# A two-layer decoder trunk on one core: the rests of the summed activations made by GpSimd instead of VectorE

## The chip, the cores and the metric

The kernel runs on one core of one Trainium2 chip. The metric is the device time of one execution in microseconds (us); a time is the median of several runs. Engine names are those of the profile: PE is TensorE, DVE is VectorE, ACT is ScalarE, POOL is GpSimd, SP is SyncE (it only issues DMAs here).

## The reference, cut to what matters

```python
D_MODEL, SEQ, DEPTH, D_FF = 1024, 512, 2, 2816

def short_conv_mixer(h, w_in, conv_w, w_out):
    b_gate, c_gate, u = jnp.split(h @ w_in, 3, axis=-1)
    y = b_gate * causal_depthwise_conv3(c_gate * u, conv_w)
    return y @ w_out

def swiglu(h, w_gate_up, w_down):
    g, u = jnp.split(h @ w_gate_up, 2, axis=-1)
    return (jax.nn.silu(g) * u) @ w_down

def reference(x, ...):
    for l in range(DEPTH):
        if l == 0:   # short convolution layer
            mix = short_conv_mixer(rmsnorm(h, a_pre_norm[l]), a_w_in[l], a_conv_w[l], a_w_out[l])
            h = h + rmsnorm(mix, a_post_norm[l])
        else:        # sliding-window attention over a shared K/V, then
            h = h + rmsnorm(attn, b_post_norm[j])
        ff = swiglu(rmsnorm(h, ffn_pre_norm[l]), ffn_w_gate_up[l], ffn_w_down[l])
        h = h + rmsnorm(ff, ffn_post_norm[l])
    return h
```

Everything is float32. 512 tokens pass through a gated convolution, a SwiGLU, an attention and a second SwiGLU.

## The kernel before, in words

**Products in three parts.** A float32 operand is written as a leading part (`hi`, in TensorE's reduced float format) and a rest (`lo` = value minus `hi`). A product is the sum of three matmuls: `hi*lo`, `hi*hi`, `lo*hi` (`mm3`, L193 to L195). So every weight tile is read from memory as `raw` (128x1024), copied by ACT to `whi` (L478) and subtracted by DVE to `wlo` (L479). Activations are split in the same way.

**Stages.** The convolution layer (to about 175 us of the trace), the first SwiGLU (about 175 to 510), the attention (to about 675), the second SwiGLU (to the end). In a SwiGLU the gate and up matrices are worked through two feature tiles at a time, a *gate pair*: a first pair in plain form and then ten in each layer, here called q0 to q9, with four down projections among them: d0 behind q2, d1 behind q4, d2 behind q6, d3 behind q9.

**A gate pair** is a fast 2x2 block product with seven products instead of eight, in the order 1, 2, 6, 5, 7, 3, 4, each a *job* with a 128x1024 weight tile. Products 1, 6, 7 and 4 accumulate in the same two banks of PSUM (`gx`, L1076 and L1079), 5 in `gz`, 3 in `gv`, 2 in `gy`. After each of them `take` (L1034) adds the bank into the running sums `st`; the next product of the `gx` chain may not start before the adds on the banks have read them. For some weights the summed blocks are made by POOL's DMAs in device memory (`hsum`, L547); in pairs q1 to q5 and q7 DVE makes two of them itself (`raw`, L466).

**The activations of a pair.** The finished pair `gr` (silu times up) goes through `pair_sums`: DVE makes the four sums of blocks `s` (L593, L594), and `split` writes each of two `s` tiles and one half of `gr` as `ahi` and `alo` (128x512 each), the stationary operands of the later down projection. The same function serves the first four column groups of the convolution's output (there the source is `yy`). In each SwiGLU the plain pair and q0 to q7 go this way (q8 and q9 go another), each during the pair that follows it; with two calls in the convolution that makes 20 calls of `pair_sums` and 60 of `split`.

**The order on each engine** is the order in which the code is written (`manual_schedule` over PE, DVE, ACT and POOL): engines take their instructions strictly in that order and wait for each other by semaphores. `in_line` runs a job's products, prepares the weights three jobs ahead (`LINE_LEAD`), and then lets one *late* step go, such as one `split` of the pair before. `issue` puts POOL's DMAs between, each held back until a named ACT copy is done ("pace").

Of the kernel before, what the change touches and what calls it, by code (L numbers as in the profile page):

```python
# [10 lines left out]
F32 = mybir.dt.float32  # L11
F32R = mybir.dt.float32r
AF = mybir.ActivationFunctionType
ALU = mybir.AluOpType
# [60 lines left out]
def yoco_kernel(  # L75
# [22 lines left out]
    nc = tc.nc  # L98
# [19 lines left out]
    def slot(s, dt=F32, w=S):  # L118
        return big.tile([P, w], dt, tag="slot", name=name(s), padded_shape=[P, S])
# [457 lines left out]
    def pair_sums(gr, to):  # L577
        v = gr.rearrange("p (k r i c) -> p k r i c", k=2, r=2, i=2)
        a11, a21, a12, a22 = v[:, 0, :, 0], v[:, 0, :, 1], v[:, 1, :, 0], v[:, 1, :, 1]
        sums = [slot("s") for _ in range(2)]  # L580
        s1, s2, s3, s4 = (p[:, c : c + 256].rearrange("p (r c) -> p r c", r=2)
                          for p in sums for c in (0, 256))
        e = slot("a11", F32R)
        h, lo = (e[:, c : c + 256].rearrange("p (r c) -> p r c", r=2) for c in (0, 256))
        t = [(e[:, :256], e[:, 256:])]
        to.append(t)

        def first():
            nc.scalar.activation(h, a11, AF.Copy)
            nc.vector.tensor_tensor(out=lo, in0=a11, in1=h.bitcast(F32), op=ALU.subtract)  # L590

        def add(p, q, u, v, w):
            nc.vector.tensor_tensor(out=p, in0=u, in1=v, op=ALU.subtract)  # L593
            nc.vector.scalar_tensor_tensor(out=q, in0=p if w is a11 else s2, scalar=-1.0,  # L594
                                           in1=w, op0=ALU.mult, op1=ALU.subtract)

        def split(src):
            hi, lo = slot("ahi", F32R), slot("alo", F32R)
            nc.scalar.activation(hi, src, AF.Copy)
            nc.vector.tensor_tensor(out=lo, in0=src, in1=hi.bitcast(F32), op=ALU.subtract)  # L600
            t.append((hi, lo))

        parts = [first, lambda: add(s1, s2, a22, a21, a11), lambda: add(s3, s4, a11, a21, a12)]
        return parts + [lambda src=src: split(src) for src in (*sums, gr[:, S:])]
# [855 lines left out]
    with tc.manual_schedule(engines=ALL):  # L1460
# [67 lines left out]
        src = [p.rearrange("p (h d) -> p h d", d=HD) for p in pv]  # L1528
        for j in range(NB):
            nc.scalar.activation(dst[j][0], src[j], AF.Copy)  # L1530
        for j in range(NB):
            if j == 2:
                qs[0].split(nc.vector)
            nc.vector.tensor_tensor(out=dst[j][1], in0=src[j], in1=dst[j][0].bitcast(F32),
                                    op=ALU.subtract)

    with tc.manual_schedule(engines=ALL):
        sum_on("a0")
        for i in range(KT + 2):
# [9 lines left out]
            for c in order.split():  # L1549
# [9 lines left out]
                op, n = c[0], [int(d) for d in c[1:].rstrip("-")]  # L1559
# [130 lines left out]
```

## Time and profile before

| | |
|---|---|
| median of three runs | 1019.07 us (1019.07 to 1019.42) |
| the profiled execution | 1018.79 us, of which 1017.0 us lie between its first and last instruction |
| granted TensorE clock | 0.999 |
| busy: PE, DVE, ACT, POOL | 1006.7, 893.3, 582.8, 195.2 us |
| idle time of PE that ends with a wait for DVE | 2.2 us on `gx`, in six places |

The table's busy times are unions over each engine's instructions. A matmul's end is modelled, so a PE that waits for a fraction of a microsecond can still read as busy; the distance between the starts of equal products shows such a wait better. Times in the trace count from the first instruction.

### The profile page before, as it was taken

To read this page: it belongs to the slowest core of one execution; us is meant where nothing else is said; L and a number is where in the kernel's file an instruction comes from. 1 tells how busy PE (TensorE), PEld (TensorE's weight loads), DVE (VectorE), ACT (ScalarE), POOL (GpSimd) and SP (SyncE) were. 2 spreads that over 40 slices of the span, in tenths; PEclk is the share of its full clock that TensorE was granted. 3 is DMA by queue.
4 is the path that set the end of the run, shared out by engine and by line. 5 is a ranking of instruction groups with operands and counts; after the bars stand their busy time and mean duration, and the time that the engine had idled before them with its cause. 6 is when DMAs were issued, how large, how long until landed. Compare 5 with 4: busy or idle time off the path is not lost.

```text
span 1017.0 us, 16055 instructions
## 1 busy us (share of the span) xinstructions
PE 1006.7 (99%) x5848; PEld 884.2 (87%) x5848; DVE 893.3 (88%) x1540; ACT 582.8 (57%) x1055; POOL 195.2 (19%) x259
## 2 busy tenths in 40 slices
PE   9999999999999999999999999999999999999997
PEld 7888888998889898898898888889988888989986
DVE  5766767899889999999888998778997999999996
ACT  7322444875656465566485786677656564655641
POOL 0443033112101011000032754131111010110001
PEclk9999999999999999999999999999999999999999
DMA  9897689549979789769504889976889677979742
GB/s 359 292 263 226 183 248 343 163 166 273 337 233 287 246 287 313 244 212 339 199 1 143 210 252 262 290 238 150 279 281 313 181 238 224 301 274 269 249 166 83
DMA packets 66575, 244.50 MB, mean 240 GB/s; under 512 B 7872, under 2 KB 8384, under 8 KB 54720
## 3 DMA queue, kind: packets, MB, share of 16 engines
q1 hardware_dynamic: 51328, 145.98, 38.7%
q0 software_dynamic: 14592, 96.48, 37.4%
q10 hardware_dynamic: 576, 1.02, 0.3%
q8 instruction: 46, 0.75, 0.3%
q14 instruction: 33, 0.27, 0.1%
HBM read 237.15 MB, written 102.76 MB: 334 GB/s over the span
## 4 chain that ended last, share of the span: by engine, by line
PE 89%; DVE 8%; issue 2%; DMA 0%; DVEq 0%; SPq 0%; ACT 0%; ACTq 0%
PE gx L1076 12%; PE gx L1079 6%; PE pcub L194 4%; PE pcub L195 4%; PE pcub L193 4%; PE px L194 4%; PE px L193 4%; PE px L195 4%; PE gz L1076 3%; PE pmix L194 3%; PE pmix L193 3%; PE pmix L195 3%; DVE wlo L479 2%; PE pz L195 2%; PE pz L194 2%
## 5 line engine op out<-in xcount | busy, mean ns | idle before, releaser
L479 DVE TENSOR_TENSOR wlo<-raw,whi 128x1024 fp32r<-128x1024 f32 x225 | 274.6, 1225 | 28.8 <-ACT whi L478 28.7
L478 ACT ACTIVATE whi<-raw 128x1024 fp32r<-128x1024 f32 x225 | 233.5, 1051 | 98.2 <-DVE raw L466 29.0
L1076 PE MATMUL gx<-xt,whi 128*128 128x512 f32 x480 | 121.6, 395 | 2.2 <-DVE st L1034 2.2
L1076 PEld LDWEIGHTS gx<-xt,whi 128*128 128x128 f32 x480 | 86.1, 189 | 19.7 <-DVE st L1034 1.7
L547 POOL DMA_DIRECT2D hsum<-in_w_gb_dram x96 | 62.9, 736 | 151.0 <-ACT whi L478 101.8
L547 POOL DMA_DIRECT2D hsum<-hsum x32 | 25.4, 793 | 296.0 <-ACT whi L478 246.4
L1034 DVE TENSOR_TENSOR st<-gx,st 128x256 f32<-128x256 f32 x200 | 77.5, 419 | 2.2 <-ACT st L1054 0.4
L1054 ACT ACTIVATE st<-gx 128x256 f32<-128x256 f32 x120 | 43.1, 380 | 60.8 <-PE gx L1079 57.6
L1079 PEld LDWEIGHTS gx<-xt,wlo 128*128 128x128 f32 x480 | 65.4, 190 | 4.8
L1079 PE MATMUL gx<-xt,wlo 128*128 128x256 f32 x480 | 66.9, 282 | 0.0
L1090 ACT ACTIVATE gr<-gr 128x1024 f32<-128x1024 f32 x20 | 21.2, 1062 | 63.6 <-DVE gr L1034 63.6
L193 PE MATMUL px<-wlo,ahi 128*128 128x512 f32 x120 | 46.7, 389 | 0.0
L194 PE MATMUL px<-whi,ahi 128*128 128x512 f32 x120 | 46.7, 389 | 0.0
L195 PE MATMUL px<-whi,alo 128*128 128x512 f32 x120 | 46.7, 389 | 0.0
L195 PE MATMUL gv<-xhi,wlo 128*128 128x256 f32 x160 | 45.3, 283 | 0.0
L193 PE MATMUL gy<-xlo,whi 128*128 128x256 f32 x160 | 45.3, 283 | 0.0
L194 PE MATMUL gy<-xhi,whi 128*128 128x256 f32 x160 | 45.3, 283 | 0.0
L193 PE MATMUL gv<-xlo,whi 128*128 128x256 f32 x160 | 45.3, 283 | 0.0
L195 PE MATMUL gy<-xhi,wlo 128*128 128x256 f32 x160 | 45.3, 283 | 0.0
L194 PE MATMUL gv<-xhi,whi 128*128 128x256 f32 x160 | 45.2, 283 | 0.0
L547 POOL DMA_DIRECT2D hsum<-in_w_dn_dram x48 | 31.7, 754 | 46.5 <-ACT whi L478 31.3
L1076 PE MATMUL gz<-xt,whi 128*128 128x512 f32 x160 | 40.1, 392 | 0.0
(298 smaller groups left out, 2923.5 us busy)
## 6 DMA issues: line engine op xcount, KB each, us to landing
hsum<-in_w_gb_dram POOLq DMA_DIRECT2D x96, 512.0 KB, 7.8
raw<-hsum SPq DMA_DIRECT2D x88, 512.0 KB, 8.1
raw<-in_w_gb_dram SPq DMA_DIRECT2D x60, 512.0 KB, 7.2
hsum<-in_w_dn_dram POOLq DMA_DIRECT2D x36, 512.0 KB, 8.2
raw<-in_w_dn_dram SPq DMA_DIRECT2D x32, 512.0 KB, 6.2
hsum<-hsum POOLq DMA_DIRECT2D x28, 512.0 KB, 5.7
raw<-in_w_in_dram SPq DMA_DIRECT2D x21, 512.0 KB, 7.9
hsum<-in_w_dn_dram POOLq DMA_DIRECT2D x12, 768.0 KB, 11.8
```

The costliest lines, as they stand in the source:

```text
L193: nc.tensor.matmul(out, whi, xlo, start=start, stop=False, **kw)
L194: nc.tensor.matmul(out, whi, xhi, start=False, stop=False, **kw)
L195: nc.tensor.matmul(out, wlo, xhi, start=False, stop=stop, **kw)
L478: self.begun = nc.scalar.activation(hi[:, :n], raw, AF.Copy)
L479: nc.vector.tensor_tensor(out=lo[:, :n], in0=raw, in1=hi[:, :n].bitcast(F32), op=ALU.subtract)
L547: nc.gpsimd.dma_start(dst, src, max_dma_last_dim=4 * 4 * S, **kw))
L1034: nc.vector.tensor_tensor(out=out, in0=a, in1=b, op=ALU.add)
L1054: nc.scalar.activation(ste, a, AF.Copy)
L1076: nc.tensor.matmul(banks[c][e], whi[:, kk], factors[p][k][2], start=opened and k == 0, stop=False, **kw)
L1079: nc.tensor.matmul(banks[c][e][:, :256], wlo[:, kk], factors[p][k][0], start=False, stop=k == 3 and p in (4, 5), **kw)
L1090: nc.scalar.activation(kept[2], kept[2], AF.Silu)
```

## The change

One instruction of `split` in `pair_sums` moves from DVE's queue to POOL's:

```diff
         def split(src):
             hi, lo = slot("ahi", F32R), slot("alo", F32R)
             nc.scalar.activation(hi, src, AF.Copy)
-            nc.vector.tensor_tensor(out=lo, in0=src, in1=hi.bitcast(F32), op=ALU.subtract)
+            nc.gpsimd.tensor_tensor(out=lo, in0=src, in1=hi.bitcast(F32), op=ALU.subtract)
             t.append((hi, lo))
```

The rows of PE, ACT and SP stay as they were. DVE has 60 rows less, POOL 60 more.

DVE while pair q1 of the first SwiGLU is worked on (`gx`, `gv`, `gz` are its banks in PSUM; the `alo` are the rests of the pair finished before it, q0; `wlo` and `raw` belong to jobs still to come), with the removed rows marked:

```order
 L1034 TENSOR_TENSOR st_451_2236<-st_452_2237,st_451_2236 128x512
 L479 TENSOR_TENSOR wlo_470_2362<-raw_426_2076,whi_469_2361 128x1024
-L600 TENSOR_TENSOR alo_473_2369<-s_448_2233,ahi_472_2368 128x512
 L1034 TENSOR_TENSOR st_452_2237<-gx_454_2239,st_452_2237 128x256 x2
 L1034 TENSOR_TENSOR st_452_2237<-gx_455_2240,st_452_2237 128x256 x2
 L479 TENSOR_TENSOR wlo_475_2393<-raw_429_2105,whi_474_2392 128x1024
-L600 TENSOR_TENSOR alo_477_2398<-s_449_2234,ahi_476_2397 128x512
 L1034 TENSOR_TENSOR gr_453_2238<-gv_478_2401,st_451_2236 128x2x256
 L479 TENSOR_TENSOR wlo_480_2428<-raw_434_2137,whi_479_2427 128x1024
 L466 TENSOR_TENSOR raw_429_2105<-raw_429_2105,raw_463_2327 128x1024
-L600 TENSOR_TENSOR alo_482_2434<-gr_417_2014,ahi_481_2433 128x512
```

The four adds on `gx` now follow the `wlo` directly, and the other steps close up in the same way.

POOL at the same place (`hsum` are the sums of weight blocks in device memory):

```order
 L547 DMA hsum_25_146<-in_w_gb_dram 64x2048
 L547 DMA hsum_26_147<-in_w_gb_dram 64x2048
+L600 TENSOR_TENSOR alo_473_2369<-s_448_2233,ahi_472_2368 128x512
 L547 DMA hsum_27_148<-in_w_gb_dram 64x2048
+L600 TENSOR_TENSOR alo_477_2398<-s_449_2234,ahi_476_2397 128x512
 L547 DMA hsum_28_149<-in_w_gb_dram 64x2048
+L600 TENSOR_TENSOR alo_482_2434<-gr_417_2014,ahi_481_2433 128x512
 L547 DMA hsum_25_146<-in_w_gb_dram 64x2048
```

POOL's queue held only paced DMAs here; the three subtractions now stand between them, and two DMAs stand behind a subtraction that they did not have to pass.

POOL in the convolution (`yy` is the gated output of two column groups, `cut` the product that the taps are taken from):

```order
 L772 TENSOR_TENSOR yy_172_534<-cut_170_532,bry_171_533 128x512
 L772 TENSOR_TENSOR yy_172_534<-cut_174_543,bry_175_544 128x512
+L600 TENSOR_TENSOR alo_188_607<-s_176_552,ahi_187_606 128x512
+L600 TENSOR_TENSOR alo_194_643<-s_177_553,ahi_193_642 128x512
+L600 TENSOR_TENSOR alo_196_647<-yy_172_534,ahi_195_646 128x512
 L759 TENSOR_TENSOR cut_180_556<-cru_179_555 128x512
```

The next column group's `cut` now has three subtractions ahead of it in POOL's queue.

## Prediction

> **What bounds the kernel now.** I read the page first (busy time, the chain that ended last), then busy time by stage, then the starts of equal products on PE, then DVE's rows in the one place where PE's starts slip.
>
> ```profile
> PE 1006.7 (99%) x5848; PEld 884.2 (87%) x5848; DVE 893.3 (88%) x1540; ACT 582.8 (57%) x1055; POOL 195.2 (19%) x259
> PE 89%; DVE 8%; issue 2%; DMA 0%; DVEq 0%; SPq 0%; ACT 0%; ACTq 0%
> 60.00:100.00 40.00, 40.00 (x179) 33.11 (x177) 26.40 (x32) 9.82 (x12) 12.41 (x15) 1.00 0.85 241
> 229.00:250.40 21.40, 20.54 (x131) 18.24 (x129) 21.23 (x36) 12.34 (x20) 4.65 (x8) 1.00 0.94 295
> 353.00:391.50 38.50, 38.50 (x253) 35.29 (x252) 37.15 (x62) 23.67 (x38) 5.21 (x8) 1.00 0.84 263
> ```
>
> The last three rows are stretches: length, then busy PE, PEld, DVE, ACT, POOL with counts, the granted clock, DMA share, GB/s. PE sets the time almost everywhere. In the convolution (60 to 100) DVE is busy for two thirds. In q5 and q6 (353 to 391.5) PE is full and DVE keeps 38.50 - 37.15 = 1.35 us free in two pairs. Only in q1 (229 to 250.4) is it the other way round: DVE 21.23 of 21.40, PE with gaps. How much PE loses there shows in the start of product 4:
>
> ```profile
> 220.56 0.40 PE L1076 MATMUL gx<-xt,whi 128*128 128x512 f32 x1
> 241.00 2.09 PE L1076 MATMUL gx<-xt,whi 128*128 128x512 f32 x8 [0.20 <-DVE st L1034]
> 262.31 2.09 PE L1076 MATMUL gx<-xt,whi 128*128 128x512 f32 x8 [0.20 <-DVE st L1034]
> 369.18 0.40 PE L1076 MATMUL gx<-xt,whi 128*128 128x512 f32 x1
> 388.90 0.40 PE L1076 MATMUL gx<-xt,whi 128*128 128x512 f32 x1
> 740.04 0.47 PE L1076 MATMUL gx<-xt,whi 128*128 128x512 f32 x1 [0.20 <-DVE st L1034]
> 761.35 0.47 PE L1076 MATMUL gx<-xt,whi 128*128 128x512 f32 x1 [0.21 <-DVE st L1034]
> ```
>
> From q5 to q6 it is 388.90 - 369.18 = 19.72 us, PE's own pace. From q0 to q1 it is 20.44, from q1 to q2 21.31: PE loses 0.72 + 1.59 = 2.31 us to DVE. The second layer repeats it (761.35 - 740.04 = 21.31). So 4.6 us in all can be won by a lighter DVE, and no more; elsewhere a lighter DVE buys nothing.
>
> **The change, part by part.** What goes from DVE and what comes to POOL (columns: count, shortest/median/longest in ns; and count, busy us, mean ns):
>
> ```profile
> L600 DVE TENSOR_TENSOR alo<-s,ahi x40: 683/685/693, 49.0 to 947.2; 128x512 fp32r<-128x512 f32 x40
> L1285 POOL TENSOR_TENSOR rhl<-ra,rhl 128x512 fp32r<-128x512 f32 x7 | 9.5, 1364 | 9.4 <-ACT rhl L1284 9.3
> ```
>
> The same subtraction of the same shape exists on POOL, in the attention: 1.36 us for 0.685. Sixty of them are 60 x 1.36 = 82 us on an engine that is busy for 195 of 1017, and 60 x 0.685 = 41 us less on DVE. The direct cost on POOL is nothing as long as nobody waits for its queue, which I come to below. The indirect one is larger: the two engines hinder each other.
>
> ```profile
> 66.61 2.33 DVE L479 TENSOR_TENSOR wlo<-raw,whi 128x1024 fp32r<-128x1024 f32 x1 [0.17 <-ACT whi L478]
> 66.58 1.29 POOL L759 TENSOR_TENSOR cut<-cru 128x512 f32<-128x512 f32 x1 [5.84 <-DVE cru L758]
> 53.10 1.22 DVE L479 TENSOR_TENSOR wlo<-raw,whi 128x1024 fp32r<-128x1024 f32 x1
> 53.32 2.16 POOL L759 TENSOR_TENSOR cut<-cru 128x512 f32<-128x512 f32 x1 [6.15 <-issue]
> 115.31 1.28 DVE L648 TENSOR_TENSOR mix<-mix,pz 128x512 f32<-128x512 f32 x2
> 116.50 1.42 DVE L479 TENSOR_TENSOR wlo<-raw,whi 128x1024 fp32r<-128x1024 f32 x1
> 115.54 1.30 POOL L772 TENSOR_TENSOR bry<-cut,bry 128x512 f32<-128x512 f32 x1 [13.40 <-DVE bry L771]
> ```
>
> A `wlo` that begins 0.03 us behind a POOL product takes 2.33 us instead of 1.22: it stands still for 1.11 us, until 1.14 us after POOL's start. A POOL product that begins 0.22 us behind a `wlo` takes 2.16 instead of 1.29: it stands still for 0.87, until 0.13 us before the `wlo` ends. Two adds with one operand in PSUM (`mix`, `pz`) run beside POOL at 0.68 each, unhindered; the `wlo` behind them waits 0.20. So whoever is first holds the other off, if DVE reads both operands from SBUF (`wlo`, `raw`, `s`, `st<-st`), and not if it reads one from PSUM (the adds on `gx`, `gz`, `gv`). The Trainium skill ("SBUF — State Buffer", section "SBUF: two separate sides") states just this as an exclusive lock on a shared port pair, held for the whole instruction; the trace agrees, with 1.11 and 0.87 us. By that rule alone, every moved subtraction shuts DVE out for longer than the 0.685 us that it took there, and the sum would turn against the change; that is the first rival below. What the rows add is that much of DVE's work has an operand in PSUM, beside which POOL costs nothing.
>
> So I walk one pair, q1, where it counts.
>
> ```profile
> 236.19 0.62 ACT L599 ACTIVATE ahi<-s 128x512 fp32r<-128x512 f32 x1
> 236.59 0.52 POOL L547 DMA_DIRECT2D hsum<-in_w_gb_dram  x1 [1.01 <-ACT whi L478]
> 236.85 0.75 DVE L1034 TENSOR_TENSOR st<-gz,st 128x256 f32<-128x256 f32 x2
> 237.63 0.69 DVE L1034 TENSOR_TENSOR st<-st,st 128x512 f32<-128x512 f32 x1
> 237.66 0.62 ACT L599 ACTIVATE ahi<-s 128x512 fp32r<-128x512 f32 x1
> 238.05 0.50 POOL L547 DMA_DIRECT2D hsum<-in_w_gb_dram  x1 [0.93 <-ACT whi L478]
> 238.24 1.22 DVE L479 TENSOR_TENSOR wlo<-raw,whi 128x1024 fp32r<-128x1024 f32 x1
> 239.13 0.62 ACT L599 ACTIVATE ahi<-gr 128x512 fp32r<-128x512 f32 x1
> 239.37 0.68 DVE L600 TENSOR_TENSOR alo<-s,ahi 128x512 fp32r<-128x512 f32 x1
> 239.98 1.67 DVE L1034 TENSOR_TENSOR st<-gx,st 128x256 f32<-128x256 f32 x4
> 241.56 1.22 DVE L479 TENSOR_TENSOR wlo<-raw,whi 128x1024 fp32r<-128x1024 f32 x1
> 242.69 0.69 DVE L600 TENSOR_TENSOR alo<-s,ahi 128x512 fp32r<-128x512 f32 x1
> 243.29 0.68 DVE L1034 TENSOR_TENSOR gr<-gv,st 128x512 f32<-128x512 f32 x1
> 243.89 1.22 DVE L479 TENSOR_TENSOR wlo<-raw,whi 128x1024 fp32r<-128x1024 f32 x1
> ```
>
> Removed from DVE's row of work: 239.98 - 239.37 = 0.61 us each, three times, 1.82 us a pair. Added, with 1.14 us of hold each:
> - The first subtraction may begin when `ahi` is done (236.81) and the DMA ahead of it issued (237.11). It falls into the adds on `gz`, holds the port until some 238.3, and `st<-st`, due at 237.63, waits 0.7 us. If DVE is earlier by then, the subtraction waits for `st<-st` and the `wlo` behind it pays 1.1.
> - The second finds the `wlo` running, waits for it, and then lies beside the four adds on `gx` (1.58 us): no wait. The 0.50 us DMA ahead of it keeps it off the port until that `wlo` is under way.
> - The third finds the next `wlo` running and then lies beside `gr<-gv` (0.60 us): the `wlo` behind that waits about 0.4.
>
> That is 1.1 to 1.5 us of waits for 1.82 saved: DVE gains 0.7 to 0.3 us in a pair. Ahead of the last slip of a layer (product 4 of q2) lie the three rests made in q0, the three in q1 and the first in q2. I take 0.7 for q0 (nothing has shifted yet), 0.3 for q1 (DVE is 0.7 earlier, the dearer case), and for the first in q2 0.61 less a wait between 0 and 0.8, so 0.2 as the middle: 1.2 us a layer, of 2.31 that can be won, 2.4 in both. The ends: waits of nothing give 4.6; waits of 1.11 for each give 7 x (1.11 - 0.61) = 3.5 us a layer of loss.
>
> Against it stand pairs where PE has little to spare. In q7 the same race comes without a DMA ahead:
>
> ```profile
> 423.43 0.62 ACT L599 ACTIVATE ahi<-s 128x512 fp32r<-128x512 f32 x1
> 424.14 1.22 DVE L479 TENSOR_TENSOR wlo<-raw,whi 128x1024 fp32r<-128x1024 f32 x1
> ```
>
> `ahi` is done at 424.05, the `wlo` begins at 424.14. If POOL is first, the adds on `gx` that product 4 waits for come 1.11 - 0.61 = 0.5 us later than now. I put 0 to 0.5 us on it in each layer, 0.25 as the middle, 0.5 in all. In the other late pairs DVE is either ahead of POOL or has the slack.
>
> What waits behind POOL: the DMAs on `hsum` and the `alo` themselves.
>
> ```profile
> hsum<-in_w_gb_dram POOLq DMA_DIRECT2D x96, 512.0 KB, 7.8
> 328.02 0.69 DVE L600 TENSOR_TENSOR alo<-s,ahi 128x512 fp32r<-128x512 f32 x1
> 337.77 0.39 PE L195 MATMUL pz<-whi,alo 128*128 128x512 f32 x1
> ```
>
> The DMAs move by one or two subtractions, some 1.4 to 2.7 us, against 7.8 us to their landing; the loads that need them come a pair or more later, so I cost that at 0. Of the `alo` this is about the tightest: 9.1 us between DVE's end and PE's first use. POOL starts about when DVE did and adds 1.36 - 0.69 = 0.7 us and a wait of 1.1; cover remains. In the convolution `cut` stands behind the three, but they are asked for from 49 us on, done by about 53.2, and `cut` began at 53.32; PE is full there and DVE has 34% free: 0.
>
> Sum: -2.4 + 0.5 = -1.9 us on the profiled 1018.79, which is 0.28 under the median of 1019.07. I predict 1017.2 as the median.
>
> **The rivals.**
> 1. *The port costs more than the subtractions did; slower.* The place is every gate pair; the price is 1.11 us of standstill per move, and it turns at 0.61. For it speaks that of the walk's rows that stay on DVE 0.69 + 3 x 1.22 = 4.35 us of 7.45 read SBUF twice, and that a waiting POOL may slip in between any two of them. Seven times 0.50 is 3.5 us a layer, 7.0 in all. Then 1.5 us a pair exceed the 0.7 that DVE has free in q3 to q8, and another 6 x 0.8 x 2 = 10 us could follow at worst: 1026 to 1036. Against it: the walk finds two of three under adds on PSUM.
> 2. *DVE is relieved in full.* Waits fall where DVE waits anyhow; PE keeps 19.72 us a pair: 1019.07 - 4.6 = 1014.5. Against it: DVE has no free 1.1 us in q1.
> 3. *Nothing moves.* Waits eat the 1.82 us to within 0.3 a pair: 1018.4 to 1019.8.
> 4. *The rests come late.* The POOL queue stands behind a DMA whose ACT copy is late, and PE waits for `alo`. It needs a delay of over 7 us; a few such would give 1021 to 1025. ACT's `whi` lies ahead of `ahi` in ACT's own queue, so I give it little.
>
> **How the numbers follow.** A measurement of this kernel tells about 0.2%, 2.0 us, from no change. Forecast (a gain of 0.7 to 3.3 us) 0.55, rival 2 0.13, rival 3 0.16, rival 1 0.13, rival 4 0.03. The forecast's 1.9 us lies close to the bound, so I give 0.27 of its 0.55 to faster; with rival 2 that is 0.40. Slower by over 2.0 us: rivals 1 and 4, 0.15 with the mildest of them left out. The rest, 0.45, is within. The forecast's own range is 1015.8 to 1018.4. Low end 1014.3: all that PE loses, 4.6 us, and 0.2 for the spread of runs. High end 1020.8: rival 3 and the mild beginnings of rival 1.
>
> **What would show it.** `alo` on POOL at about 1.3 us, up to 2.4 where it met a `wlo`; `wlo` with a mean over 1.23 us; product 4 from q1 to q2 in less than 21.31 us (20.8 or so, if I am right); 19.72 unchanged from q5 to q6. Wrong, if that last distance grows (rival 1), if q1 to q2 stays at 21.31 (rival 3) or falls to 19.7 (rival 2), or if PE waits for POOL at all (rival 4).

## The result, and the profile after

The changed kernel takes 1023.62 us (median of five runs, 1023.4 to 1023.84) against 1019.07 us; the ratio is 1.0045, with a 95% interval of 1.003 to 1.006. It is slower by 4.5 us, outside the range and on the other side than forecast.

The page of the changed kernel, the line of busy times and two groups (line, engine, operation, tiles, count, busy us, mean ns, idle before):

```profile
PE 1006.7 (99%) x5848; PEld 883.9 (87%) x5848; DVE 890.1 (87%) x1480; ACT 582.1 (57%) x1055; POOL 292.7 (29%) x319
L479 DVE TENSOR_TENSOR wlo<-raw,whi 128x1024 fp32r<-128x1024 f32 x225 | 303.1, 1352 | 32.9 <-ACT whi L478 32.5
L600 POOL TENSOR_TENSOR alo<-s,ahi 128x512 fp32r<-128x512 f32 x40 | 63.4, 1590 | 59.3 <-ACT ahi L599 59.1
```

The `wlo` group on the page before the change:

```profile
L479 DVE TENSOR_TENSOR wlo<-raw,whi 128x1024 fp32r<-128x1024 f32 x225 | 274.6, 1225 | 28.8 <-ACT whi L478 28.7
```

Sixty instructions have left DVE, but its busy time fell by 3.2 us only (893.3 to 890.1). The `wlo` alone grew from 274.6 to 303.1 us: the same work, with standstill inside it. On POOL a subtraction of an `s` tile takes 1.59 us in the mean.

Where PE lost it shows in the starts of product 4, the rows that answer to those of the prediction:

```profile
221.16 0.63 PE L1076 MATMUL gx<-xt,whi 128*128 128x512 f32 x2
242.69 0.47 PE L1076 MATMUL gx<-xt,whi 128*128 128x512 f32 x1 [1.64 <-DVE st L1034]
264.26 0.47 PE L1076 MATMUL gx<-xt,whi 128*128 128x512 f32 x1 [1.61 <-DVE st L1034]
721.89 0.40 PE L1076 MATMUL gx<-xt,whi 128*128 128x512 f32 x1
744.30 0.47 PE L1076 MATMUL gx<-xt,whi 128*128 128x512 f32 x1 [1.42 <-DVE st L1034]
765.65 0.47 PE L1076 MATMUL gx<-xt,whi 128*128 128x512 f32 x1 [1.40 <-DVE st L1034]
```

From q0 to q1 and from q1 to q2 it is now 21.53 and 21.57 us (20.44 and 21.31 before), in the second layer 22.41 and 21.35 (20.45 and 21.31 before). With PE's own pace of 19.73 taken off, the first layer waits 3.6 us instead of 2.3 and the second 4.3 instead of 2.3: +3.3 us together. Another 0.35 us in each layer comes up between q4 and q5, where DVE's lateness from q4 is carried into d1 and PE waits for the adds on `mix`; smaller ones follow behind q5. In all, the last product 4 of the program starts 4.8 us later than before and the first 0.6 us later, so 4.2 us come up between them. The first 0.6 us is not counted to the change: 0.54 of it is there already when PE starts its product on `pr` (32.95 us against 32.41), and the first subtraction on GpSimd begins at 49.8 us. This start-up differs from run to run (in run 2 below, whose convolution is the old one, the first product 4 came at 221.67).

VectorE's and GpSimd's rows in q1 of the changed kernel:

```profile
237.57 1.30 POOL L600 TENSOR_TENSOR alo<-s,ahi 128x512 fp32r<-128x512 f32 x1
238.81 0.52 POOL L547 DMA_DIRECT2D hsum<-in_w_gb_dram  x1
239.34 1.31 POOL L600 TENSOR_TENSOR alo<-s,ahi 128x512 fp32r<-128x512 f32 x1
241.12 1.75 POOL L600 TENSOR_TENSOR alo<-gr,ahi 128x512 fp32r<-128x512 f32 x1
237.70 1.73 DVE L1034 TENSOR_TENSOR st<-st,st 128x512 f32<-128x512 f32 x1
239.35 2.39 DVE L479 TENSOR_TENSOR wlo<-raw,whi 128x1024 fp32r<-128x1024 f32 x1
241.67 1.66 DVE L1034 TENSOR_TENSOR st<-gx,st 128x256 f32<-128x256 f32 x4
```

`st<-st` stands still for 1.73 - 0.69 = 1.04 us behind the first subtraction, the `wlo` for 2.39 - 1.22 = 1.17 behind the second. The adds on `gx`, for which PE's product 4 waits, begin at 241.67, 1.69 us later than before (239.98), although DVE had begun this stretch at the same time (237.70 against 237.63). Only the third subtraction lies beside the adds; in this pair it costs VectorE nothing.

### The profile page after: what moved, and what is told of

Its sections match the earlier page's. It is cut to its first block, busy times and chain, and to the rows that moved or that the text cites. A ratio compares the mean times of both kernels' runs of the same rounds, so it can differ in the third digit from the quotient of the medians.

```text
span 1021.8 us, 16117 instructions
## 1 busy us (share of the span) xinstructions
PE 1006.7 (99%) x5848; PEld 883.9 (87%) x5848; DVE 890.1 (87%) x1480; ACT 582.1 (57%) x1055; POOL 292.7 (29%) x319
## 4 chain that ended last, share of the span: by engine, by line
PE 81%; DVE 10%; issue 4%; DMA 2%; ACT 2%; POOL 0%; DVEq 0%; SPq 0%; ACTq 0%
PE gx L1076 11%; PE gx L1079 5%; PE px L193 4%; PE px L194 4%; PE px L195 4%; PE pcub L193 3%; PE pcub L194 3%; PE pcub L195 3%; PE pmix L194 3%; PE pmix L193 3%; PE pmix L195 3%; DVE wlo L479 3%; PE gz L1076 3%; DMA raw<-in_w_in_dram 2%; DVE st L1034 2%
## 5 line engine op out<-in xcount | busy, mean ns | idle before, releaser
L479 DVE TENSOR_TENSOR wlo<-raw,whi 128x1024 fp32r<-128x1024 f32 x225 | 303.1, 1352 | 32.9 <-ACT whi L478 32.5
L1076 PE MATMUL gx<-xt,whi 128*128 128x512 f32 x480 | 121.1, 394 | 6.7 <-DVE st L1034 6.7
L1076 PEld LDWEIGHTS gx<-xt,whi 128*128 128x128 f32 x480 | 86.2, 189 | 23.3 <-issue 6.8
L600 POOL TENSOR_TENSOR alo<-s,ahi 128x512 fp32r<-128x512 f32 x40 | 63.4, 1590 | 59.3 <-ACT ahi L599 59.1
L300 POOL TENSOR_TENSOR ur<-uv,mhalf 128x1 f32<-128x1 f32 x15 | 13.9, 928 | 122.1 <-DVE uv L296 122.0
```

The lines of the kernel that those rows point to most:

```text
L479: nc.vector.tensor_tensor(out=lo[:, :n], in0=raw, in1=hi[:, :n].bitcast(F32), op=ALU.subtract)
L600: nc.gpsimd.tensor_tensor(out=lo, in0=src, in1=hi.bitcast(F32), op=ALU.subtract)
L1076: nc.tensor.matmul(banks[c][e], whi[:, kk], factors[p][k][2], start=opened and k == 0, stop=False, **kw)
```

## The experiments

The theories: **port** (DVE stands still while GpSimd reads SBUF; what counts is which instruction of DVE the read meets, and whether PE waits for what stands behind that one; runs 5 to 9 call it the phase theory) against **queue** (POOL's queue delays DMAs or rests, or the loss begins in the convolution). Later the second rival became **count**: each moved subtraction costs what the port takes, wherever it falls. Every edit below is made to the changed kernel. Added lines shift its line numbers, so L479 there is L481 in some of these kernels, and L1076 is L1078 or L1084.

**1 and 2. One stage alone.** `pair_sums` gets the engine as an argument:

```diff
-    def pair_sums(gr, to):
+    def pair_sums(gr, to, eng):
...
-            nc.gpsimd.tensor_tensor(out=lo, in0=src, in1=hi.bitcast(F32), op=ALU.subtract)
+            eng.tensor_tensor(out=lo, in0=src, in1=hi.bitcast(F32), op=ALU.subtract)
```

The first kernel passes `nc.gpsimd` in the convolution alone:

> Only the six subtractions of the convolution are made by GpSimd, the 54 of the two SwiGLUs by VectorE. Port theory (VectorE stands still while GpSimd reads SBUF, and PE pays only where the adds on gx are late): in the convolution PE is full and VectorE has a third free, so 1019.1, within 0.6 us. Rival (the loss begins in the convolution, where the trace after is 0.6 us late at the first gate pair, and is carried on): 1019.7 to 1021.

Measured: 1018.97 us, ratio 1.000 (0.999 to 1.001). The second passes it in the SwiGLUs alone:

> Only the 54 subtractions of the SwiGLUs by GpSimd. Port theory: nearly all of the loss, 1023.0 to 1023.6, with product 4 from q1 to q2 again 21.6 us apart and the slips in q4 and q5. Rival (the loss begins in the convolution): 1021 to 1022.

Measured: 1023.3 us, ratio 1.0042 (1.0027 to 1.0057). The whole loss is in the SwiGLUs; the convolution hides its six.

**3. The relief alone.**

```diff
-            nc.gpsimd.tensor_tensor(out=lo, in0=src, in1=hi.bitcast(F32), op=ALU.subtract)
-            t.append((hi, lo))
+            t.append((hi, hi))
```

> All 60 subtractions are left out of both engines; the matmuls that read a rest read the leading part instead, so PE does the same work. This is VectorE's relief alone. Both theories: PE's 4.6 us of waits in q1 and q2 go, 1014.5 (1014.0 to 1015.5). If it stays at 1017 or more, VectorE's load was not what PE waited for, and the whole reckoning of the prediction is off.

Measured: 1013.96 us, ratio 0.995 (0.9935 to 0.9965), 5.1 us less and just under the expected range. PE waits for DVE on `gx` nowhere any more. So DVE's load was what PE waited for, and the most that a move could win is 5 us. The half microsecond beyond 4.6 lies outside q0 to q2: from q8 to q9 product 4 now takes 19.73 us instead of 19.88, and from q2 to q3 48.29 instead of 48.37, in both layers.

**4. GpSimd as busy, but without a read.**

```diff
-            nc.gpsimd.tensor_tensor(out=lo, in0=src, in1=hi.bitcast(F32), op=ALU.subtract)
+            for _ in range(3):
+                nc.gpsimd.memset(lo.bitcast(F32), 0.0)
```

> In place of each subtraction GpSimd writes zeros three times into the same tile, 3 x 0.52 = 1.6 us, with no read of SBUF (the result lacks the rests). VectorE is relieved as in the run before it, GpSimd's queue is as full as after the change. Port theory (it is GpSimd's reads that shut VectorE out): wlo keeps 1.22 us, 1014.5 to 1015.5. Rival (GpSimd's queue: DMAs that stand behind the new work, or rests that come late): 1021 to 1024.

Measured: 1013.85 us, ratio 0.995 (0.9935 to 0.9964), 0.65 us under the expected range. GpSimd's and VectorE's rows in q1, and the `wlo` group of this kernel's page:

```profile
PE 1004.9 (99%) x5848; PEld 884.6 (87%) x5848; DVE 863.1 (85%) x1480; ACT 587.0 (58%) x1055; POOL 287.8 (28%) x439
237.83 1.72 POOL L601 MEMSET alo<- 128x512 f32 x3
237.62 1.22 DVE L479 TENSOR_TENSOR wlo<-raw,whi 128x1024 fp32r<-128x1024 f32 x1
239.98 1.72 POOL L601 MEMSET alo<- 128x512 f32 x3
240.34 1.22 DVE L479 TENSOR_TENSOR wlo<-raw,whi 128x1024 fp32r<-128x1024 f32 x1
L479 DVE TENSOR_TENSOR wlo<-raw,whi 128x1024 fp32r<-128x1024 f32 x225 | 274.2, 1224 | 37.5 <-ACT whi L478 37.1
```

POOL is as busy as after the change (287.8 against 292.7 us), its DMAs stand behind as much work, and the writes lie beside `wlo` without lengthening it. It is the reads. One part of the queue theory is not covered here: a memset does not wait for ACT's `ahi`, while in the changed kernel POOL, and the DMAs behind it, waited 67 us for that in all. Run 8 covers it: there POOL waits 106 us for `wlo` alone ahead of its subtractions, and the kernel is faster than the one before. So the queue theory falls. DVE at 863.1 against 890.1 us gives the standstill as 27 us over the whole program, 0.45 us a move.

**5 and 6. A third of the move, at two phases.** Only one of the three subtractions goes to GpSimd (`i` counts them):

```diff
-            nc.gpsimd.tensor_tensor(out=lo, in0=src, in1=hi.bitcast(F32), op=ALU.subtract)
+            eng = nc.gpsimd if i in (2,) else nc.vector
+            made = eng.tensor_tensor(out=lo, in0=src, in1=hi.bitcast(F32), op=ALU.subtract)
```

> Of the three subtractions of a call only the third (the half of gr) is made by GpSimd, 20 in all. Phase theory (what counts is beside which VectorE instruction the read falls): with the first two on VectorE, the third becomes ready in q1 at about 239.8, just ahead of the four adds on gx, which read PSUM; it lies beside them and nobody waits, so VectorE gains 0.61 us in a pair ahead of product 4: about 0.61 x 2 a layer, 2.4 in all, 1016.7 (1015.5 to 1017.8). Count theory (each moved subtraction costs about as much port time as it saves, wherever it falls): a third of the change's loss of 4.5 us, 1020.5.

Measured: 1020.83 us, ratio 1.0015 (1.0007 to 1.0024): the number of the count theory, not mine. The trace has both:

```profile
240.79 1.29 POOL L601 TENSOR_TENSOR alo<-gr,ahi 128x512 fp32r<-128x512 f32 x1
240.74 1.67 DVE L1036 TENSOR_TENSOR st<-gx,st 128x256 f32<-128x256 f32 x4
447.40 1.29 POOL L601 TENSOR_TENSOR alo<-gr,ahi 128x512 fp32r<-128x512 f32 x1 [10.93 <-ACT ahi L599]
447.70 2.08 DVE L479 TENSOR_TENSOR wlo<-raw,whi 128x1024 fp32r<-128x1024 f32 x1
448.02 0.40 PE L1078 MATMUL gx<-xt,whi 128*128 128x512 f32 x1
468.64 0.40 PE L1078 MATMUL gx<-xt,whi 128*128 128x512 f32 x1
```

In q1 the read lies beside the four adds on `gx`, as expected, and from q1 to q2 product 4 takes 20.71 us, just 0.60 less than before the change. But in q8 the same instruction runs ahead of a `wlo`, which stands still for 0.86 us, and from q8 to q9 it is 20.62 us where it was 19.88 (447.40 to 467.28 in the kernel before). Smaller slips from q0 to q1 and behind q4 and q6 are added. I had walked one pair and counted it for all.

With `(0,)` in place of `(2,)`, the first subtraction alone:

> Only the first subtraction of a call by GpSimd, 20 in all. Phase theory: in q1 it is ready at about 237.2, beside the adds on gz, and runs into st<-st, which waits 0.7 to 1.04 us ahead of the adds on gx; 0.61 is saved, so PE loses 0.1 to 0.4 us more in each of q1 and q2: 1019.2 to 1021. Count theory: as with the third alone, 1020.5; the two kernels come out alike.

Measured: 1018.55 us, ratio 0.9993 (0.9984 to 1.0002), a tie, and below what I expected. The rows in q1:

```profile
237.53 1.32 POOL L601 TENSOR_TENSOR alo<-s,ahi 128x512 fp32r<-128x512 f32 x1
237.58 1.83 DVE L1036 TENSOR_TENSOR st<-st,st 128x512 f32<-128x512 f32 x1
```

`st<-st` does stand still for 1.14 us, but product 4 slips about as much as before the change (20.37 us from q0 to q1 and 21.33 from q1 to q2, against 20.44 and 21.31), and the slips in the later pairs are absent. The two kernels move the same number of subtractions of the same shape and lie 2.3 us apart, against the count theory.

**7. The same instruction, held back.** The first subtraction waits for the `wlo` that stands ahead of it in the program:

```diff
+    newest = []
...
+            newest.append(nc.vector.tensor_tensor(out=lo[:, :n], in0=raw, ...))
...
+            if i in (0,) and newest:
+                tc.add_manual_dep(made.ins, newest[-1].ins.name, mybir.DependencyInfo(
+                    mybir.DependencyClass.Sync, mybir.DependencyReason.DATA), reason="pace")
```

> As the run before, but the first subtraction on GpSimd also waits for the wlo that stands ahead of it in the program, so that it begins with the four adds on gx. The same work on the same engines; only the phase differs. Phase theory: no wait of VectorE in q1 and q2, 0.61 us gained in each ahead of product 4, twice or three times a layer: 1015.5 to 1016.8. Count theory: 1020.5 again. Rival (a later rest is waited for by PE): over 1021.

Measured: 1015.54 us, ratio 0.9965 (0.9953 to 0.9977). One added wait turns a tie into a gain of 3.7 us. The rows in q1:

```profile
237.83 1.22 DVE L481 TENSOR_TENSOR wlo<-raw,whi 128x1024 fp32r<-128x1024 f32 x1
239.19 1.30 POOL L604 TENSOR_TENSOR alo<-s,ahi 128x512 fp32r<-128x512 f32 x1 [2.04 <-DVE wlo L481]
238.96 1.67 DVE L1042 TENSOR_TENSOR st<-gx,st 128x256 f32<-128x256 f32 x4
240.55 1.22 DVE L481 TENSOR_TENSOR wlo<-raw,whi 128x1024 fp32r<-128x1024 f32 x1
```

POOL begins 0.23 us behind the adds and is done with the port before the next `wlo`, which keeps 1.22 us. This is the phase, shown by itself: same work, same engines, another start.

**8. All three held back** (the same edit with `(0, 1, 2)`):

> All three subtractions on GpSimd, each held back until the wlo ahead of it in the program is done. Phase theory: the first lies beside the adds on gx (no wait), the second beside gr<-gv with 0.5 us of wait behind it, the third meets the sum of raw blocks or the products on st and costs 0.5 to 1.1; 1.0 to 1.7 of wait for 1.82 saved, and none of it ahead of the adds on gx: 1015.5 to 1018. Count theory: as after the change, 1023.6.

Measured: 1015.37 us, ratio 0.9963 (0.995 to 0.9975). This is 0.1 us under the expected range. The move as a whole, which loses 4.5 us unpaced, gains 3.9 us with the three waits; the slip from q0 to q1 is gone.

```profile
242.68 2.01 DVE L481 TENSOR_TENSOR wlo<-raw,whi 128x1024 fp32r<-128x1024 f32 x1
244.61 1.21 DVE L468 TENSOR_TENSOR raw<-raw,raw 128x1024 f32<-128x1024 f32 x1
242.31 1.30 POOL L604 TENSOR_TENSOR alo<-s,ahi 128x512 fp32r<-128x512 f32 x1 [0.95 <-DVE wlo L481]
244.86 2.12 POOL L604 TENSOR_TENSOR alo<-gr,ahi 128x512 fp32r<-128x512 f32 x1 [0.78 <-DVE wlo L481]
```

The second costs 0.8 us of standstill for 0.61 saved, since `gr<-gv` beside it is short. So it is left on VectorE.

**9. First and third held back, the second on VectorE** (`(0, 2)`):

> The first and the third subtraction on GpSimd, each held back until the wlo ahead of it in the program is done; the second on VectorE. Phase theory: the first lies beside the adds on gx at no cost, the third behind the sum of raw blocks and beside two adds on gx, with 0.3 us of wait behind it; the second, which cost 0.8 us of wait for 0.61 saved when all three were held back, stays. 1.22 saved less 0.3 is 0.9 us in a pair, against 0.6 with the first alone and 0.7 with all three: 1014.5 to 1015.4. Count theory: between the kernels with one and with three, 1015.4 to 1015.6.

Measured: 1014.57 us, ratio 0.9956 (0.9943 to 0.997), inside the expected range. It has the lowest time of the kernels here that make all the rests, 4.6 us under the kernel before, and 0.6 above the run without any rest. Its interval overlaps that of run 8, so it is the trace that tells the two apart: product 4 from q1 to q2 takes 19.87 us here and 20.29 there.

```profile
220.87 0.40 PE L1084 MATMUL gx<-xt,whi 128*128 128x512 f32 x1
240.60 0.40 PE L1084 MATMUL gx<-xt,whi 128*128 128x512 f32 x1
260.47 0.40 PE L1084 MATMUL gx<-xt,whi 128*128 128x512 f32 x1
244.10 2.12 POOL L604 TENSOR_TENSOR alo<-gr,ahi 128x512 fp32r<-128x512 f32 x1 [2.82 <-DVE wlo L481]
245.77 1.60 DVE L1066 SCALAR_TENSOR_TENSOR gr<-st,gr 128x512 f32<-128x512 f32 x2
```

Product 4 comes after 19.73 and 19.87 us, PE's own pace but for 0.14. The third subtraction waits for the sum of raw blocks itself and costs 1.60 - 1.29 = 0.3 us behind it.

## Why the prediction was wrong, by its own steps

- **What can be won: nearly right.** 4.6 us were read from the starts of product 4; without the subtractions the kernel was 5.1 us faster. That "elsewhere a lighter DVE buys nothing" missed the half microsecond that run 3 shows outside q0 to q2.
- **The price of a meeting: right.** 1.11 us had been read from one `wlo`; the changed kernel shows 1.04 and 1.17. So was the exemption of adds that read PSUM. The Trainium skill ("SBUF — State Buffer", section "SBUF: two separate sides") confines the lock to a VectorE instruction with two SBUF inputs against a GpSimd instruction that reads SBUF; run 4 agrees, where the `wlo` keeps a mean of 1.224 us beside GpSimd's writes. The rule is thus narrower than "every moved subtraction shuts DVE out".
- **The walk of q1, second subtraction: the step that failed.** "The second finds the `wlo` running, waits for it": it began at 239.34, 0.01 us ahead of the `wlo`, and shut it out for 1.17 us. The prediction had let the first subtraction push `st<-st` back, but not seen that this pushes the `wlo` to just where the second, one DMA of 0.52 us later, is ready. Waits ahead of product 4 were put at 0.7 to 1.1 us in q1; they were 2.21, for 0.61 saved in q1 up to there.

The forecast's sum can be redone with the measured waits. These rows of the changed kernel, first layer, belong to q0 and q2; those of q1 stand with the result:

```profile
220.24 2.00 DVE L479 TENSOR_TENSOR wlo<-raw,whi 128x1024 fp32r<-128x1024 f32 x1
222.77 1.70 DVE L479 TENSOR_TENSOR wlo<-raw,whi 128x1024 fp32r<-128x1024 f32 x1
259.43 1.59 DVE L1034 TENSOR_TENSOR st<-st,st 128x512 f32<-128x512 f32 x1
260.95 2.37 DVE L479 TENSOR_TENSOR wlo<-raw,whi 128x1024 fp32r<-128x1024 f32 x1
```

| what DVE gains up to product 4 of q2, in us (saved less waits) | forecast | first layer | second layer |
|---|---|---|---|
| q0, three subtractions | 0.7 | 1.82 - 1.26 = 0.56 | 1.82 - 2.56 = -0.74 |
| q1, three subtractions | 0.3 | 1.82 - 2.21 = -0.39 | 1.82 - 1.81 = 0.01 |
| q2, what lies ahead of product 4 | 0.2 | 0.61 - 2.05 = -1.44 | 0.61 - 1.85 = -1.24 |
| sum | 1.2 | -1.3 | -2.0 |
| product 4 from q0 to q2, before less after | | -1.35 | -2.0 |

A wait is what a row lasts beyond 1.22 us (`wlo`) or 0.69 us (`st<-st`); those of the second layer are the rows at 720.97, 739.71, 740.97, 761.03 and 762.39 us. The sum comes out at what PE lost. In the first layer the two waits behind the second subtraction, 1.17 in q1 and 1.15 in q2, are the difference: without them the sum is 1.05, near the forecast. The second layer has them too (1.17 and 1.10), and the 2.56 us in q0 that is shown at the end.

- **The relief was forecast rightly in kind, but fell where PE has no use for it.** Over the program VectorE was 3.2 us less busy. In q0 to q2, where PE waits for DVE, the waits ahead of product 4 were more than the savings, by the table. Behind product 4 of q2, where PE did not wait for DVE (48.34 us to the next product 4, 48.37 before), three subtractions made one `wlo` stand still for 1.12 us (293.56 us, lasting 2.34) against 1.82 saved.
- **The race in q7: wrong place.** There DVE kept the port and product 4 did not slip. "In the other late pairs DVE is either ahead of POOL or has the slack" failed instead: in q4 POOL began 0.13 us behind a `wlo` (rows below) and still had the port first, which cost 1.32 us; the next `wlo` stood still for 0.78 more. DVE was late from there into d1, and PE lost 0.35 us by q5. I had taken the start stamps for the order at the port.
- **The convolution, the lateness of `alo`, the DMAs behind POOL: right**, all nothing (run 1 for the convolution, runs 4 and 8 for the queue; PE waited for no `alo`).
- **Rival 1** named the mechanism and the direction that came. Its price held only where a read met an instruction with both operands in SBUF: in the mean the standstill was 0.45 us a move, below its turning point of 0.61. What turned the change against PE was where the meetings fell, in q0 to q2 and around q4. So its time of 1026 to 1036 was too high.

## What to carry to other kernels

Before work is moved from VectorE to GpSimd, it pays to look at what each instruction reads: where VectorE read both operands from SBUF in these runs, it and a reading GpSimd instruction took turns, and what the move saved could be given back. Here the same move lost 4.5 us or gained 3.9 depending on when GpSimd began; for the first subtraction, a dependency on the VectorE instruction just ahead of work on PSUM put it in the right place. A walk through one pair was not enough, for the forecast or for run 5: the same instruction met another neighbour in other pairs. And busy time saved on an engine counts only if it is saved ahead of the instruction that the bounding engine waits for.

## What the runs showed of the hardware that I had not expected

The earlier start in the trace is not always the one that gets the port. Two cases of the changed kernel, q4 and q7:

```profile
328.86 2.54 DVE L479 TENSOR_TENSOR wlo<-raw,whi 128x1024 fp32r<-128x1024 f32 x1
328.99 1.31 POOL L600 TENSOR_TENSOR alo<-s,ahi 128x512 fp32r<-128x512 f32 x1
426.56 1.22 DVE L479 TENSOR_TENSOR wlo<-raw,whi 128x1024 fp32r<-128x1024 f32 x1
426.56 3.65 POOL L600 TENSOR_TENSOR alo<-s,ahi 128x512 fp32r<-128x512 f32 x2 [2.34 <-ACT ahi L599]
```

In q4 POOL, right behind a DMA issue, began 0.13 us after the `wlo` and was not hindered (1.31 us), while the `wlo` took 2.54. In q7 POOL came out of a wait, began with the `wlo` to 0.01 us, and it was POOL that waited. Whether coming out of a wait is what decides was not tried.

VectorE can also lose twice in a row. In q0 of the second layer a `wlo` took 3.78 us, two whole subtractions longer than its 1.22, while POOL ran them one behind the other:

```profile
720.97 3.78 DVE L479 TENSOR_TENSOR wlo<-raw,whi 128x1024 fp32r<-128x1024 f32 x1
721.11 1.30 POOL L600 TENSOR_TENSOR alo<-s,ahi 128x512 fp32r<-128x512 f32 x1
722.36 1.29 POOL L600 TENSOR_TENSOR alo<-gr,ahi 128x512 fp32r<-128x512 f32 x1
```

That is where the second layer lost 0.9 us more than the first from q0 to q1.
